# A two-layer mixer trunk on one core: the pooled branch added by accumulating DMAs in six of eight merged tiles of layer 2, and the tiles' first differences tied to an earlier matmul

## The chip, the cores and the metric

The kernel runs on one core of one Trainium2 chip. A time is the device time of one execution in microseconds (us), and the figure that counts is the median over several runs. Times inside an execution come from one profiled run and count from the start of its span. The engines are named as the profile names them: PE (matmul) with PEld (its weight loads), DVE (vector), ACT (scalar), POOL (GpSimd) and SP, which only issues DMAs here.

## The reference

A residual stream of 512 tokens, 16 meta tokens ahead of them and 1024 features passes two layers. Each layer normalises it, projects it, runs a pooled branch and a latent attention branch side by side, gates the two, adds them, and projects the sum back:

```python
y_pool = (pool_mix(u_pool, ...) * silu(z_pool)) @ pool_w_up[l]
o_mla = mla(c_q, c_kv, k_rope, pos, ...)
y_mla = (o_mla * silu(z_mla)) @ mla_w_up[l]
merged = jax.nn.sigmoid(g_pool) * y_pool + jax.nn.sigmoid(g_mla) * y_mla
h_res = h_res + merged @ w_out[l]
```

After layer 2 the meta tokens are dropped. The `+` in `merged` is what this case is about.

## The kernel before

Features lie on the 128 partitions and tokens along a row, so the 1024 features are eight tiles. In layer 2 a merged tile is 128 x 512 (the meta tokens are no longer needed). Every matrix product is done in three matmuls of reduced-precision operands: weight and input are each split into a high part and a low rest, and `mm3` (lines 188, 191 and 192 of `kernel.py`) multiplies high by high, high weight by low input, low weight by high input. The split of a weight chunk is one ACT copy (`whi`, line 183) and one DVE subtraction (`wlo`, line 184); the split of an input tile is the same pair in the helper `split` (lines 297 and 298).

Weights come in 128 x 512 chunks of 256 KB through SP's DMA queue (line 115) into three `raw` buffers (a few into `kh` and `kl`). A `raw` buffer is free for the next chunk when its `wlo` is done, so a late `wlo` on DVE makes a later weight late.

The order of the work. `stream` walks a list of products and yields after each group of matmuls with its estimated length; the list's order is fixed in `register`. `go` is the layer's script: `up(name)` emits products until the named one is done, `fill_now(ns)` emits about that many nanoseconds of matmuls, and in between it emits the work of the other engines. The final order on each engine is then set by the scheduler of the tile framework. Each engine takes its instructions in that order and waits at the first one whose inputs are not there; DMAs are issued by an engine's own queue in the same way. `behind(a, b)` adds a wait of `a` for `b` without a use of data, and `newest[0]` is the last matmul emitted so far. A wait on `newest[0]` thus keeps DVE work from being put too early.

The end of layer 2, where the change is:

- **Products mu0 to mu7** (weights `wmu`, input the attention branch `ogs`, in the profile `q` and `kn`). Each fills a PSUM tile `mm`. Its end is `ev_mu(m)`: line 1049 turns the gate tile `gms[m]` (named `cq`) into (gate + 1) x product, line 1052 adds the gated pooled branch `am[m]`, and `split` makes the inputs `hh`, `hl` of the output product. `am[m]` lives in `xb[:, m]`.
- **`residual(m)`**, eight DMAs on POOL's queue (line 1108), load the residual stream into `xb[:, m]`. Each must wait until `am[m]` there has been read.
- **Output products.** o0, o1, o2 and o3 have a product of their own each, of 24 matmuls of 512 columns. The other four output tiles, in two pairs, are made by `out_pairs`: seven half-size products (256 columns) instead of eight, from sums and differences of weights (prepared earlier, `wsum`) and of the merged tiles. `blend(p)` makes the latter, for p = 7, 6, 5, 4 in turn: for p = 7 tile k minus tile k+4, for k = 0 to 3 (line 1091), for p = 6 lines 1095 and 1096, for p = 4 line 1103. Their splits go into tiles `sq`, `rinv`, `cq` and `u`.
- **Carried halves.** ACT copies some PSUM results out of the banks named `S` into `sv` (line 1130), and POOL adds `sv` to `xb` by accumulating DMAs (line 1131). The outputs `yT` go out on POOL's and SP's queues (line 1068).

In `go` the end reads: all mu products, the eight residual loads, then for each p a `fill_now(2600)` and a blend, then the rest.

Of the kernel before, what the change touches and what calls it, by code (L numbers as in the profile page):

```python
# [14 lines left out]
ALU = mybir.AluOpType  # L15
# [8 lines left out]
T = SEQ + NM  # L24
# [48 lines left out]
def trunk(ctx, tc, xT, pos, win, wkr, wqb, wkb, wvb, wgr, wpu, wmu, wout, gains, const, yT):  # L73
    nc = tc.nc
    pe, act, dve, gp, sp = nc.tensor, nc.scalar, nc.vector, nc.gpsimd, nc.sync
# [66 lines left out]
    def other_loads(made):  # L142
        for k, m in ((2, 0), (4, 1), (6, None)):
            ins = sp.dma_start(xb[:, k:k + 2, :T], xT[:, k:k + 2, :])
            behind(ins, made)
            if m is not None:
                raw = rawt()
                behind(sp.dma_start(raw, win[0, MT_CKV + m, :, 512:1024]), made)
                early.append(raw)
        behind(sp.dma_start(cst, const), made)  # L150
        behind(sp.dma_start(posb[:, :T], pos.partition_broadcast(P)), made)
        dve.tensor_copy(maskw[:, 512 - P:], cst[:, C_MASK:C_MASK + P])
        dve.tensor_copy(identr, ident)
# [97 lines left out]
    def step():  # L251
        c = next(main, None)
        if c is None:
            flush()
            return False
        clk[0] += c
        while pend and pend[0][0] <= clk[0]:
            pend.pop(0)[1]()
        return True

    def after(ns, fn):
        pend.append((clk[0] + ns, fn))
        pend.sort(key=lambda e: e[0])

    def ready():
        while pend and pend[0][0] <= clk[0] + 12000.0:
            pend.pop(0)[1]()
# [5 lines left out]
    def upto(name):  # L273
        while name not in done:
            if not step():
                break
# [10 lines left out]
    def fill_now(ns):  # L287
        end = clk[0] + ns
        while clk[0] < end and step():
            pass  # L290
# [5 lines left out]
    def split(hi, lo, src, a, b):  # L296
        act.activation(hi[:, a:b], src, AF.Copy)  # L297
        dve.tensor_sub(lo[:, a:b], src, hi[:, a:b].bitcast(F32))  # L298
# [42 lines left out]
    def weight_sums(name, w):  # L341
        def made(u, i):
            a, b = w[2 * u], w[2 * u + 1]
            d = wsum[name][u]
            src = {0: (b[:, 0:512], b[:, 512:1024]), 2: (a[:, 0:512], b[:, 0:512]), 1: (a[:, 0:512], d[:, 0, :]),
                   3: (a[:, 512:1024], d[:, 1, :])}
            return d[:, i, :], src[i]

        def copy(d, src):
            behind(sp.dma_start(d, src[0]), earlier(14000))  # L350

        def add(d, src):
            behind(gp.dma_start(d, src[1], accum_op=ALU.add), earlier(4000))  # L353

        for u in range(len(w) // 2):
            for fn, i in ((copy, 0), (copy, 2), (add, 0), (copy, 1), (add, 2), (add, 1), (copy, 3), (add, 3)):
                yield lambda fn=fn, u=u, i=i: fn(*made(u, i))

    class Layer:
# [684 lines left out]
        def ev_mu(self, m):  # L1044
            def ev(ps, a, b):
                if a == self.x0:
                    self.mg[m] = self.hs[m]
                t = self.gms[m][:, a:b]
                dve.scalar_tensor_tensor(out=t, in0=t, scalar=1.0, in1=ps, op0=ALU.add, op1=ALU.mult)
                if b == T:  # L1050
                    t, x0 = self.gms[m], self.x0
                    dve.tensor_add(t[:, x0:T], t[:, x0:T], self.am[m][:, x0:T])
                    split(*self.mg[m], t[:, x0:T], x0, T)
            return ev

# [200 lines left out]
        def go(self, nxt):  # L1256
            l = self.l
            up = lambda name: upto((l, name))
            mix = iter(range(99))
            if l == 0:  # L1260
                for k in range(8):
                    if k in (0, 1, 3, 5):
                        step()
                    self.split_h(k)
                    if k == 0:
                        other_loads(first)
            up("ckv1")
            if l == 0:
                for k in range(8):
                    self.square_x(k)  # L1270
            self.norm_sums()
            up("u1")
            for m in range(2):
                self.mix(m, self.window(m))
            up("u3")
            s2 = self.window(2)
            up("k3")
            s3 = self.window(3)
            up("zp0")
            self.mix(2, s2)  # L1280
            up("zp1")
            self.mix(3, s3)
            self.k_factors()
            if l == 0:
                sums = [*weight_sums(0, [wout[0, m] for m in OUT]), *weight_sums("gp", [win[1, MT_GP + m] for m in range(8)])]
                for i, fn in enumerate(sums):
                    after(3850 * (i + 1), fn)
            up("qr1")
            for s, (a, b) in enumerate(FULL):
                a0 = max(a, self.x0)  # L1290
                self.stat(self.acc[:, a0:b], a0, b, C_CQ, self.acc_last)
            up("qn3")
            self.qk_stats()
            if l == 0:
                fill_now(2600)
            kq = self.prep(0)
            if l == 1:
                for i, fn in enumerate(weight_sums(1, [wout[1, m] for m in OUT])):
                    after(4500 * (i + 1), fn)
            fill_now(2600)  # L1300
            due[0] = None
            prev = None
            for h in range(H):
                kn_ = self.head(h, kq, prev, lambda: self.mixed(next(mix)))
                self.gap()
                self.mixed(next(mix))
                if h + 1 < H:
                    kq = self.prep(h + 1)
                self.pv(prev, (2, 3))
                prev = kn_  # L1310
                self.gap()
                self.mixed(next(mix))
            fill_now(1300)
            self.pv(prev, (0, 1))
            fill_now(2600)
            if not self.last:
                self.meta_queries()
            self.pv(prev, (2, 3))
            up("gm6")
            if self.last:  # L1320
                self.gates_again()
            up("gm7")
            ready()
            if not self.last:
                for p in range(4):
                    self.meta_out(p)
            up("mu7")
            for m in range(8):
                self.residual(m)
            for p in (7, 6, 5, 4):  # L1330
                fill_now(2600)
                self.blend(p)
            up("ob")
            if nxt is not None:
                for k in range(8):
                    nxt.split_h(k)
# [76 lines left out]
```

## Time and profile before

| | us |
|---|---|
| median of 3 runs | 786.03 |
| lowest, highest | 784.74, 787.63 |
| the profiled execution, its own time | 788.06 |
| its span in the profile | 786.2 |

The profiled execution took 2.03 us more than the median, and 1.86 us of its time lie around the span. The granted TensorE clock was 1.0. In the page's first part PE is busy for 774.8 us of the span, DVE for 587.0 and POOL for 230.2. In a timeline row stand start, length, engine, line, operation, output<-input, shape and count; in brackets the idle time ahead of it on its engine and what ended it. A row's length includes a tail that overlaps the next instruction, so the step from start to start is what an instruction costs an engine that is never idle.

### The profile page before, as it was taken

To read this page: it belongs to the slowest core of one execution; us is meant where nothing else is said; L and a number is where in the kernel's file an instruction comes from. 1 tells how busy PE (TensorE), PEld (TensorE's weight loads), DVE (VectorE), ACT (ScalarE), POOL (GpSimd) and SP (SyncE) were. 2 spreads that over 40 slices of the span, in tenths; PEclk is the share of its full clock that TensorE was granted. 3 is DMA by queue.
4 is the path that set the end of the run, shared out by engine and by line. 5 is a ranking of instruction groups with operands and counts; after the bars stand their busy time and mean duration, and the time that the engine had idled before them with its cause. 6 is when DMAs were issued, how large, how long until landed. Compare 5 with 4: busy or idle time off the path is not lost.

```text
span 786.2 us, 15369 instructions
## 1 busy us (share of the span) xinstructions
PE 774.8 (99%) x5469; PEld 711.1 (90%) x5469; DVE 587.0 (75%) x1316; ACT 446.7 (57%) x1022; POOL 230.2 (29%) x319
## 2 busy tenths in 40 slices
PE   9999999999999999999999999999999999999998
PEld 8999899999999999999997898887788899788887
DVE  5848788547778977689764477775997899974984
ACT  8545655645556665545664356455667676654462
POOL 1024514203434342211320245131026235240213
PEclk9999999999999999999999999999999999999999
DMA  6242367765645465565653423435456566562655
GB/s 243 82 97 87 103 163 165 180 154 136 144 120 138 120 135 150 135 187 155 172 151 92 102 81 95 125 88 181 121 132 162 160 168 164 150 212 88 213 148 136
DMA packets 64909, 110.76 MB, mean 141 GB/s; under 512 B 10544, under 2 KB 16560, under 8 KB 64832
## 3 DMA queue, kind: packets, MB, share of 16 engines
q1 hardware_dynamic: 54928, 90.02, 38.4%
q0 software_dynamic: 8896, 17.92, 12.6%
q10 hardware_dynamic: 1008, 1.84, 0.6%
q8 instruction: 43, 0.70, 0.4%
q14 instruction: 34, 0.28, 0.1%
HBM read 100.18 MB, written 22.62 MB: 156 GB/s over the span
## 4 chain that ended last, share of the span: by engine, by line
PE 84%; DVE 6%; DMA 4%; issue 2%; ACT 2%; POOL 0%; SPq 0%; DVEq 0%; ACTq 0%
PE mm L188 24%; PE mm L192 23%; PE mm L191 23%; DVE wlo L184 2%; PE S L188 2%; PE S L191 2%; PE S L192 2%; PE mm L946 2%; DMA raw<-wsumgp 1%; DMA raw<-win 1%; PE o L952 1%; PE o L951 1%; PE S L500 1%; ACT whi L183 1%; DMA raw<-wqb 1%
## 5 line engine op out<-in xcount | busy, mean ns | idle before, releaser
L188 PE MATMUL mm<-hh,whi 128*128 128x264 f32 (+2 forms) x992 | 306.0, 311 | 1.6 <-DVE tmp L637 0.6
L192 PE MATMUL mm<-hh,wlo 128*128 128x264 f32 (+2 forms) x992 | 304.1, 309 | 1.1 <-DVE wlo L184 1.0
L191 PE MATMUL mm<-hl,whi 128*128 128x264 f32 (+2 forms) x992 | 304.5, 308 | 0.0
L184 DVE TENSOR_TENSOR wlo<-raw,whi 128x512 fp32r<-128x512 f32 (+2 forms) x261 | 191.9, 739 | 98.1 <-ACT whi L183 94.3
L183 ACT ACTIVATE whi<-raw 128x512 fp32r<-128x512 f32 (+2 forms) x261 | 156.5, 603 | 165.9 <-PE mm L191 91.0
L188 PEld LDWEIGHTS mm<-hh,whi 128*128 128x128 f32 x992 | 186.2, 188 | 12.9 <-issue 1.2
L192 PEld LDWEIGHTS mm<-hh,wlo 128*128 128x128 f32 x992 | 185.8, 188 | 10.6 <-DVE wlo L184 2.3
L191 PEld LDWEIGHTS mm<-hl,whi 128*128 128x128 f32 x992 | 186.8, 188 | 9.1
L188 PE MATMUL mm<-cq,whi 128*128 128x264 f32 (+2 forms) x140 | 44.2, 316 | 1.3 <-ACT racc L960 0.7
L192 PE MATMUL mm<-cq,wlo 128*128 128x264 f32 (+2 forms) x140 | 43.5, 313 | 0.6 <-DVE wlo L184 0.6
L191 PE MATMUL mm<-cq,whi 128*128 128x264 f32 (+2 forms) x140 | 43.5, 312 | 0.0
L879 DVE CUSTOM_DVE_ANT_0 S<-S,maskw,nqs 128x288 f32<-128x288 f32 (+4 forms) x80 | 38.4, 497 | 2.5 <-PE S L192 2.2
L702 POOL TENSOR_TENSOR racc<-racc,tmp 128x264 f32<-128x264 f32 (+1 forms) x15 | 14.3, 951 | 87.2 <-ACT tmp L701 87.1
L188 PE MATMUL mm<-u,whi 128*128 128x264 f32 (+1 forms) x108 | 35.3, 327 | 0.1
L192 PE MATMUL mm<-u,wlo 128*128 128x264 f32 (+1 forms) x108 | 34.8, 322 | 0.0
L298 DVE TENSOR_TENSOR tl<-mm,th 128x512 fp32r<-128x512 f32 (+1 forms) x64 | 29.2, 481 | 7.4 <-ACT th L297 6.3
L850 POOL TENSOR_TENSOR tmp<-kp,bc 64x528 f32<-64x528 f32 x16 | 25.6, 1602 | 30.5 <-issue 15.4
L353 POOL DMA_DIRECT2D wsum<-wout x8 | 6.9, 859 | 89.0 <-PE mm L192 73.0
L924 POOL TENSOR_TENSOR pm<-pa,rs 128x16 f32<-128x16 f32 x32 | 11.0, 345 | 72.6 <-DVE rs L919 66.7
L926 POOL TENSOR_TENSOR cq<-cq,rs 128x384 f32<-128x384 f32 (+1 forms) x32 | 32.2, 1005 | 0.0
L886 ACT ACTIVATE cq<-S,bia 128x400 f32<-128x400 f32 (+2 forms) x48 | 24.6, 515 | 12.2 <-DVE bia L914 7.2
L297 ACT ACTIVATE th<-mm 128x512 fp32r<-128x512 f32 (+1 forms) x64 | 25.9, 432 | 8.4 <-PE mm L946 7.3
(333 smaller groups left out, 1722.0 us busy)
## 6 DMA issues: line engine op xcount, KB each, us to landing
raw<-win SPq DMA_DIRECT2D x139, 256.0 KB, 3.0
raw<-wout SPq DMA_DIRECT2D x22, 256.0 KB, 3.5
bc<-kdr SPq DMA_DIRECT2D x16, 264.0 KB, 4.2
wsum<-wout SPq DMA_DIRECT2D x16, 256.0 KB, 3.5
raw<-wpu SPq DMA_DIRECT2D x16, 256.0 KB, 3.1
wsumgp<-win SPq DMA_DIRECT2D x16, 256.0 KB, 3.3
raw<-wmu SPq DMA_DIRECT2D x16, 256.0 KB, 2.7
raw<-wsumgp SPq DMA_DIRECT2D x16, 256.0 KB, 3.8
```

The costliest lines, as they stand in the source:

```text
L183: act.activation(hi[:, :n], raw[:, :n], AF.Copy)
L184: dve.tensor_sub(lo[:, :n], raw[:, :n], hi[:, :n].bitcast(F32))
L188: first = pe.matmul(out, wh, xh, start=start, stop=False, skip_group_check=more)
L191: pe.matmul(out, wh, xl, start=False, stop=False, skip_group_check=more)
L192: newest[0] = pe.matmul(out, wl, xh, start=False, stop=stop, skip_group_check=more)
L297: act.activation(hi[:, a:b], src, AF.Copy)
L298: dve.tensor_sub(lo[:, a:b], src, hi[:, a:b].bitcast(F32))
L850: gp.tensor_mul(kf[r0:r0 + 64, :], self.kp[r0:r0 + 64, :], bc[r0:r0 + 64, :])
L879: dve.tensor_tensor_reduce(out=sv, in0=sv, in1=mask, scale=nqs[:, i, h:h + 1], scalar=3e38, op0=ALU.add, op1=ALU.min, accum_out=bia[:, c:c ...
L886: act.activation(pv, sv, AF.Exp, scale=-1.0, bias=bia[:, i:i + 1], accum_out=rs[:, c:c + 1])
L926: gp.tensor_mul(pt[i][:, NM:], pt[i][:, NM:], rs[:, i:i + 1].to_broadcast([P, n - NM]))
L946: pe.transpose(tr[:, P * (i - j):P * (i - j + 1)], pt[i][:, NM + P * j:NM + P * (j + 1)], ident)
```

## The change

Only layer 2 (`self.last`) changes. For merged tiles 0 to 5 the DVE addition of the pooled branch becomes an accumulating DMA on POOL's queue, from SBUF to SBUF, 256 KB each; tiles 6 and 7 keep the DVE addition. And the `fill_now(2600)` ahead of `blend(7)` is left out, so that the differences are tied to the last matmul of mu7 rather than to one of o0, and each later blend to a matmul one such step older.

```diff
                 if b == T:
                     t, x0 = self.gms[m], self.x0
-                    dve.tensor_add(t[:, x0:T], t[:, x0:T], self.am[m][:, x0:T])
+                    if self.last and m < 6:
+                        gp.dma_start(t[:, x0:T], self.am[m][:, x0:T], accum_op=ALU.add)
+                    else:
+                        dve.tensor_add(t[:, x0:T], t[:, x0:T], self.am[m][:, x0:T])
                     split(*self.mg[m], t[:, x0:T], x0, T)
...
             for p in (7, 6, 5, 4):
-                fill_now(2600)
+                if p != 7 or not self.last:
+                    fill_now(2600)
                 self.blend(p)
```

The lines behind the edits move by 3 and 4: 1091 becomes 1094, 1095 becomes 1098, 1108 becomes 1111, 1130 becomes 1133.

What follows is the order of instructions, without times. On POOL's queue, at the end of layer 2, there stood eight residual loads in a row, each behind the DVE addition of its tile. Of the changed kernel these are the rows at that place (line 1053 is the accumulating DMA, and `cq_1885`, `1886`, `1887`, `1888`, `1889`, `1890` are merged tiles 0 to 5; line 1111 the residual load):

```order
L1053 DMA cq_1885_9611<-xb 128x512
L1053 DMA cq_1886_9613<-xb 128x512
L1053 DMA cq_1887_9615<-xb 128x512
L1111 DMA xb<-scr 128x512
L1053 DMA cq_1888_9617<-xb 128x512
L1111 DMA xb<-scr 128x512
L1053 DMA cq_1889_9619<-xb 128x512
L1111 DMA xb<-scr 128x512 x3
L1053 DMA cq_1890_9621<-xb 128x512
L1111 DMA xb<-scr 128x512 x3
```

The first residual load waits for tile 0's accumulating DMA to land, the second for tile 1's; the three in one row are those of tiles 2, 3 and 6, which wait for tile 2's and tile 3's DMAs and tile 6's DVE addition. The DMA of tile 3 stands behind the first residual load, that of tile 5 behind the three.

On DVE, around the last mu products, the kernel before has these rows (`mm_9824` is mu7; `cq_1874` and `cq_1894` are merged tiles 6 and 7; `hl` the low parts; line 1091 the differences of p = 7):

```order
L1049 SCALAR_TENSOR_TENSOR cq_1894_9647<-cq_1894_9647,mm_9824 128x512
L184 TENSOR_TENSOR wlo_10084<-kl_10081,whi_10083 128x512
L298 TENSOR_TENSOR hl_15_141<-cq_1889_9619,hh_14_140 128x512
L1052 TENSOR_TENSOR cq_1890_9621<-cq_1890_9621,xb 128x512
L1052 TENSOR_TENSOR cq_1894_9647<-cq_1894_9647,xb 128x512
L298 TENSOR_TENSOR hl_19_145<-cq_1874_9577,hh_18_144 128x512
L184 TENSOR_TENSOR wlo_9926<-raw_9923,whi_9925 128x512
L184 TENSOR_TENSOR wlo_9961<-raw_9958,whi_9960 128x512
L298 TENSOR_TENSOR hl_17_143<-cq_1890_9621,hh_16_142 128x512
L298 TENSOR_TENSOR hl_21_147<-cq_1894_9647,hh_20_146 128x512
L1091 TENSOR_TENSOR cq_1889_9619<-cq_1885_9611,cq_1889_9619 128x256
```

The changed kernel has at the same place:

```order
L1049 SCALAR_TENSOR_TENSOR cq_1894_9647<-cq_1894_9647,mm_9824 128x512
L298 TENSOR_TENSOR hl_15_141<-cq_1889_9619,hh_14_140 128x512
L1094 TENSOR_TENSOR cq_1874_9577<-cq_1887_9615,cq_1874_9577 128x256
L184 TENSOR_TENSOR wlo_10084<-kl_10081,whi_10083 128x512
L1055 TENSOR_TENSOR cq_1894_9647<-cq_1894_9647,xb 128x512
L1094 TENSOR_TENSOR cq_1889_9619<-cq_1885_9611,cq_1889_9619 128x256
L298 TENSOR_TENSOR hl_21_147<-cq_1894_9647,hh_20_146 128x512
L298 TENSOR_TENSOR sq_9850<-cq_1889_9619,sq_9849 128x256
L1094 TENSOR_TENSOR cq_1894_9647<-cq_1888_9617,cq_1894_9647 128x256
L184 TENSOR_TENSOR wlo_9942<-raw_9939,whi_9941 128x512
L298 TENSOR_TENSOR hl_17_143<-cq_1890_9621,hh_16_142 128x512
```

The addition for tile 5 is gone from DVE, `hl_17_143` (tile 5's low part) now waits for a DMA, and three of the four differences stand ahead of it.

On PE, at the products of p = 7 and p = 6 of the pairs, the kernel before has (`mm_10149` and `mm_10129` are the banks of p = 7; the `S` banks those of p = 6, reused after an ACT copy of line 1130):

```order
L188 MATMUL mm_10149<-sq_9880,whi_10125 128x256
L191 MATMUL mm_10149<-sq_9881,whi_10125 128x256
L188 MATMUL S_10043<-cq_1952_9895,whi_10145 128x256
L191 MATMUL S_10043<-u_1953_9896,whi_10145 128x256
L188 MATMUL S_10065<-cq_1952_9895,whi_10165 128x256
```

and the changed kernel:

```order
L191 MATMUL mm_10149<-sq_9858,whi_10125 128x256
L192 MATMUL mm_10149<-sq_9857,wlo_10126 128x256
L188 MATMUL mm_10149<-sq_9861,whi_10125 128x256
L191 MATMUL mm_10149<-sq_9862,whi_10125 128x256
L192 MATMUL mm_10149<-sq_9861,wlo_10126 128x256
L188 MATMUL S_10043<-cq_1945_9864,whi_10145 128x256
L191 MATMUL S_10043<-u_1946_9865,whi_10145 128x256
```

Ten more matmuls of `mm_10149` (all twelve of that product) now stand ahead of the first matmul into the reused `S` bank.

## Prediction

> **What bounds the kernel now.** The page first: its first part says which engine is full, the chain of waits which one set the end.
>
> ```profile
> PE 774.8 (99%) x5469; PEld 711.1 (90%) x5469; DVE 587.0 (75%) x1316; ACT 446.7 (57%) x1022; POOL 230.2 (29%) x319
> ...
> PE 84%; DVE 6%; DMA 4%; issue 2%; ACT 2%; POOL 0%; SPq 0%; DVEq 0%; ACTq 0%
> ```
>
> PE is busy for 774.8 of 786.2 us. The change takes no matmul away, so it can win only PE's idle time, and of that only what lies behind the edit. The view of busy time by stretches, laid over the end of layer 2 (busy time and count for PE, PEld, DVE, ACT and POOL, then granted clock, DMA share and GB/s), shows how much that is:
>
> ```profile
> 726.50:738.70 12.20, 12.20 (x55) 9.87 (x54) 12.15 (x21) 6.23 (x11) 2.55 (x5) 1.00 0.57 187
> 738.70:750.00 11.30, 11.30 (x50) 9.14 (x49) 8.82 (x15) 4.73 (x8) 1.86 (x4) 1.00 0.68 219
> 750.00:760.00 10.00, 10.00 (x63) 8.93 (x62) 10.00 (x27) 7.04 (x17) 1.10 (x2) 1.00 0.33 96
> 760.00:770.00 10.00, 8.84 (x72) 8.43 (x72) 10.00 (x24) 5.97 (x14) 3.98 (x6) 1.00 0.71 197
> 770.00:780.00 10.00, 10.00 (x63) 8.95 (x63) 4.11 (x7) 2.44 (x5) 3.90 (x7) 1.00 0.57 118
> ```
>
> DVE is full from 726.5 to 738.7, and again from 750 to 770. PE does not care, except in one stretch: 760 to 770, where it is idle for 1.16 us. The timeline finds the two places:
>
> ```profile
> 762.81 0.38 PE L188 MATMUL S<-cq,whi 128*128 128x256 f32 x1 [0.92 <-ACT sv L1130]
> ...
> 768.77 0.39 PE L188 MATMUL S<-cq,whi 128*128 128x256 f32 x1 [0.24 <-ACT sv L1130]
> ```
>
> Both are the first matmul into an `S` bank that ACT must empty first. Why ACT was late at the first place, by the timelines of ACT, SP and DVE:
>
> ```profile
> 761.86 0.63 ACT L183 ACTIVATE whi<-raw 128x512 fp32r<-128x512 f32 x1 [1.96 <-DMA raw<-wsum]
> 762.39 0.64 ACT L1130 ACTIVATE sv<-S 128x256 f32<-128x256 f32 x2
> ...
> 751.81 7.41 SPq L115 DMA_DIRECT2D raw<-wsum  x3
> ...
> 756.24 0.69 DVE L184 TENSOR_TENSOR wlo<-raw,whi 128x512 fp32r<-128x512 f32 x1
> ```
>
> The copies of line 1130 stand behind a weight copy that waited for its DMA. That DMA could go only once DVE had freed its buffer, at 756.24 + 0.69 = 756.93, and landed about 4.9 us later. So DVE's backlog after 750 is what PE paid for, and the prize is **1.16 us** at most.
>
> **The DVE side of the change.** The timeline of DVE where the additions stand, and where the differences do:
>
> ```profile
> 726.55 1.28 DVE L1049 SCALAR_TENSOR_TENSOR cq<-cq,mm 128x512 f32<-128x512 f32 x2 [2.88 <-PE mm L192]
> 727.76 0.68 DVE L184 TENSOR_TENSOR wlo<-raw,whi 128x512 fp32r<-128x512 f32 x1
> 728.36 0.69 DVE L1052 TENSOR_TENSOR cq<-cq,xb 128x512 f32<-128x512 f32 x1
> 728.96 0.68 DVE L1049 SCALAR_TENSOR_TENSOR cq<-cq,mm 128x512 f32<-128x512 f32 x1
> ...
> 749.74 1.43 DVE L1091 TENSOR_TENSOR cq<-cq,cq 128x256 f32<-128x256 f32 x4 [2.48 <-PE mm L192]
> ...
> 752.36 0.42 DVE L298 TENSOR_TENSOR sq<-cq,sq 128x256 fp32r<-128x256 f32 x1
> 752.70 0.42 DVE L1095 TENSOR_TENSOR cq<-cq 128x256 f32<-128x256 f32 x1
> ```
>
> From start to start a 512-column instruction costs a full DVE 0.60 us, a 256-column one 0.34. Six additions less are 6 x 0.60 = 3.6 us of DVE between 728 and 743, but PE is not idle there, so by itself this wins nothing. The second edit matters more: the differences waited 2.48 us for a matmul of o0, with DVE idle, just ahead of its backlog. They now need only mu7 and their own tiles, and go into that hole. The second blend takes over the first one's matmul, the low-weight product of o0 with tile 5. PE's rows give the pace:
>
> ```profile
> 738.65 0.40 PE L192 MATMUL mm<-q,wlo 128*128 128x512 f32 x1
> 738.88 0.39 PE L188 MATMUL mm<-hh,whi 128*128 128x512 f32 x1
> ...
> 755.57 0.28 PE L188 MATMUL S<-hh,whi 128*128 128x256 f32 x1
> 755.69 0.28 PE L191 MATMUL S<-hl,whi 128*128 128x256 f32 x1
> ```
>
> A 512-column matmul takes 0.232 us of PE (72 of them from 738.88 to 755.57), a 256-column one 0.118. In the new order that matmul is the 36th of the output products: 738.88 + 35 x 0.232 + 0.4 = 747.4. From there DVE has nineteen instructions ahead of the `wlo` that frees the buffer, sixteen of 256 columns and three of 512: 16 x 0.34 + 3 x 0.60 = 7.2, so it starts at 754.6 instead of 756.24. The weight then lands near 760.2, and ACT's copies of `S`, 0.53 + 0.64 us on, end near 761.4. PE wants the bank at 762.81 - 0.92 = 761.9 plus the ten matmuls that moved ahead of it, 1.2 us: 763.1. The 0.92 us go, with 1.7 us to spare, and the 0.24 behind them, on the same engines, I count as gone too. No other idle time of PE is late next: PE is the bound up to the last product, whose order the change leaves.
>
> **The POOL side.** Each removed addition becomes a DMA, and three things queue up. On ACT, the copy `hh` of a tile waits for the landing, and weight copies stand behind it. On DVE, `hl` waits for `hh`, and `wlo` rows stand behind it. On POOL, the residual load of a tile waits for the landing of that tile's DMA, and the DMA of a later tile stands behind the load. That makes a chain: tile 0 lands, its residual load goes, tile 3's DMA goes and lands, three residual loads go (the third waits for tile 6's addition on DVE), tile 5's DMA goes and lands. PE waits for tile 5.
>
> No row shows this very DMA: 256 KB, added from SBUF to SBUF. The nearest, by the answers on lines 1131 (`xb<-sv`, added from SBUF to SBUF, but 128 or 132 KB) and 353 (256 KB, added in DRAM), and a plain load on POOL's queue:
>
> ```profile
> L1131 POOL DMA_DIRECT2D xb<-sv x12: 862/893/1178, 380.7 to 776.6; - x12
> ...
> DMA to landing us min/median/max: 2.7/3.8/5.1
> ...
> DMA to landing us min/median/max: 4.2/5.6/7.6
> ...
> 729.41 0.62 POOL L1108 DMA_DIRECT2D xb<-scr  x1 [30.76 <-DVE cq L1052]
> ```
>
> The first landing row belongs to line 1131, the second to line 353. So the landing takes from 2.7 us (half the bytes) to 7.6 us (the worst in DRAM). It also depends on company. The queues:
>
> ```profile
> q1 hardware_dynamic: 54928, 90.02, 38.4%
> q0 software_dynamic: 8896, 17.92, 12.6%
> ```
>
> POOL's queue takes 12.6% of 786.2 us for 17.92 MB, 5.5 us of all sixteen engines per MB, so 1.4 us for each new DMA and 8.7 us for six. From 726.5 to 750 the DMA engines are busy for 12.2 x 0.57 + 11.3 x 0.68 = 14.6 of 23.5 us; with the new ones 23.3, nearly full. I take 4.0 us for tile 0, which starts where the engines are still idle, and 5.5 us, next to the DRAM median, for tiles 3 and 5.
>
> Now the sum. Line 1049 of tile 0 ends at 727.24, so its DMA goes at 727.3. Tile 5 lands at 727.3 + 4.0 + 0.6 (a residual load's issue) + 5.5 + 2 x 0.6 + 5.5 = 744.1. PE wants `hh` of tile 5 as the 30th matmul, at 738.88 + 29 x 0.232 = 745.6; an ACT copy takes 0.6, so the tile must land by 744.9. Only 0.8 us are to spare, and ACT and DVE carry weight copies between, so I charge 0.3 us of stall. In other words: tile 5 lands at 729.1 plus three landings, and PE begins to stall when the three exceed **15.8 us**.
>
> By the Trainium skill ("DMA: Bandwidth & Descriptors", section on the anatomy of one DMA on the SWDGE path) a DMA of POOL's queue takes about 2.0 us plus its bytes over 436 GB/s: 2.6 us for 256 KB as an estimate, 7.8 for the chain, and the full 1.16 us would be won. The trace disagrees for adding DMAs: the best of line 353's took 4.2 us and the median 5.6, and the measurement decides.
>
> **Sum.** 788.06 - 1.16 + 0.3 = 787.2 for an execution like the profiled one, which lies 2.03 above the median. On the scale of the medians: 786.03 - 0.86, so **785.2 us**.
>
> **The rivals.**
>
> *The gain is given back.* At 5.6 us for each of the three, the DRAM median, the sum is 16.8, one us over the point, and the tiles' copies on ACT lose some tenths more; net 0 to -0.2: 786.0. The same time results if the differences bring nothing, because the weight is late for another reason, such as full DMA engines. For this speaks the DMA sum of 23.3 in 23.5 us; against it that the first DMA starts in a quiet stretch, and that line 1131's, from SBUF, land faster.
>
> *The chain on POOL makes it slower.* One landing beyond 15.8 us in sum is one us of PE stall, since nothing behind PE can make it up; beyond 15.8 + 1.16 = 17.0, a mean of 5.7 us, the kernel is slower than before. At a mean of 6.0: 18 - 15.8 - 1.2 = +1.0, 787.0; at the worst row's 7.6: 22.8 - 15.8 - 1.2 = +5.8, 791.8.
>
> *POOL is hindered by DVE.* Were descriptors written more slowly while DVE works, each issue would lengthen; the longest of line 1131's is 1.18 us against a median of 0.89, so 0.3 on each of three links, 0.9 in sum, which just uses up the 0.8 to spare: 785.5. Against it: with DVE busy for 12.15 of 12.20 us, POOL's five issues took 2.55 us, 0.51 each. The Trainium skill ("GPSIMD Engine Reference", section 1, Specifications) has GpSimd contend with DVE instructions of two SBUF inputs, as all of these are; by that rule this rival holds, and the trace's plain loads do not agree.
>
> **How the numbers follow.** The forecast, -1.2 to -0.4 with the third rival in it: 0.50. Given back, -0.4 to +0.5: 0.25. Slower by 0.5 to 3.9 us: 0.16. Slower by more than 3.9 us, 0.5% and about what a measurement of this kernel can tell from no change: 0.07, for which the mean landing must pass 6.9 us. Faster by more than 3.9 us: 0.02, as PE has only 1.16 us to give. So 0.02, 0.91 and 0.07. The range ends above at a mean landing near 6.5 us (19.5 - 15.8 - 1.2 = +2.5), below at the full gain, 784.9; the runs of before spread from 784.74 to 787.63, so I allow the median of a few runs 0.9 on the lower side: **784.0 to 788.5**.
>
> **What would show it.** Right: between 760 and 770 PE's busy time is 10.0; the first blend's rows carry no wait for PE and lie ahead of 747; the adding DMAs land in 4 to 5.5 us. Wrong: a wait of PE between 743 and 749 for `hh` or `hl` of a tile or for a weight copy behind one; landings of 6 us or more; POOL's residual loads waiting for them; or a new wait of PE near 767, where the `S` banks are reused a second time.

## The result, and the profile after

The changed kernel takes **791.05 us** (median of six runs, 789.33 to 792.59) against 785.71 for the kernel before beside it (six runs, 784.74 to 787.63): the ratio is 1.0065, 95% interval 1.0053 to 1.0077. It is slower by 5.3 us; 785.2 was predicted, with a range to 788.5.

The profiled execution took 791.76 us, with a span of 789.6. The first instruction of the place in question, line 1049 of tile 0, starts at 726.87 instead of 726.55, before anything differs. From there to the end of the span it is 62.7 us, before 59.65: **the tail is 3.1 us longer** in this execution. The view by stretches, as shown of before (busy time and count for PE, PEld, DVE, ACT and POOL, granted clock, DMA share, GB/s):

```profile
726.50:738.70 12.20, 12.20 (x54) 9.90 (x53) 9.04 (x15) 5.36 (x9) 6.21 (x8) 1.00 0.79 174
738.70:750.00 11.30, 8.41 (x33) 5.58 (x31) 8.84 (x17) 5.36 (x10) 3.63 (x6) 1.00 1.01 299
...
760.00:770.00 10.00, 10.00 (x79) 9.69 (x78) 9.03 (x21) 5.79 (x12) 2.37 (x3) 1.00 0.76 207
770.00:780.00 10.00, 9.47 (x60) 8.41 (x59) 4.73 (x8) 4.25 (x9) 4.32 (x6) 1.00 0.57 132
```

The 1.16 us between 760 and 770 are gone, as forecast, but PE now stands for 2.9 us between 738.7 and 750, where the DMA engines are full (1.01 of their time by this view), and for 0.5 us after 770. PE's timeline has the three places before 750:

```profile
741.98 0.73 PE L188 MATMUL mm<-hh,whi 128*128 128x512 f32 x2 [0.52 <-ACT hh L297]
...
748.60 0.50 PE L188 MATMUL mm<-hh,whi 128*128 128x512 f32 x1 [2.10 <-ACT whi L183]
...
749.61 1.02 PE L188 MATMUL mm<-hh,whi 128*128 128x512 f32 x2 [0.27 <-ACT hh L297]
```

The chain of work that ended last is now this (start, length, what); before, it ran along PE here:

```profile
727.97 4.71 DMA cq<-xb
732.72 0.59 issue
733.30 0.56 POOL xb L1111
733.86 7.41 DMA cq<-xb
741.27 0.40 issue
741.67 1.08 POOL xb L1111 x2
742.76 6.14 DMA cq<-xb
748.92 0.64 ACT hh L297
749.61 0.49 PE mm L188
```

It is the chain on POOL that the prediction describes: tile 0 lands, a residual load goes, tile 3's DMA goes and lands, residual loads go, tile 5's DMA goes and lands. Its three landings are 4.7, 7.4 and 6.1 us, 18.3 in sum. At its end PE starts tile 5's first matmul, the 30th of the output products, at 749.61. The first of them started at 739.20, so without a wait the 30th would have come at 739.20 + 29 x 0.232 = 745.9: **PE is 3.7 us late there**. (Idle times in the rows add up to only 2.9, because the matmuls next to a wait also take 0.34 or 0.52 us instead of 0.23.) The answer on line 1053 gives all six:

```profile
DMA to landing us min/median/max: 4.7/6.6/7.4
```

The longest of PE's waits, 2.10 us, came another way, through tile 4. It lies inside the 3.7: an earlier tile 4 would only have let PE wait longer for tile 5. Rows of POOL, ACT and DVE in order of time:

```profile
737.08 0.88 POOL L1053 DMA_DIRECT2D cq<-xb  x1 [1.03 <-DVE hl L298]
744.16 0.63 ACT L297 ACTIVATE hh<-cq 128x512 fp32r<-128x512 f32 x1 [1.20 <-DMA cq<-xb]
744.83 0.69 DVE L298 TENSOR_TENSOR hl<-cq,hh 128x512 fp32r<-128x512 f32 x1 [0.38 <-ACT hh L297]
745.44 0.42 DVE L1094 TENSOR_TENSOR cq<-cq,cq 128x256 f32<-128x256 f32 x1
745.77 0.68 DVE L184 TENSOR_TENSOR wlo<-kl,whi 128x512 fp32r<-128x512 f32 x1
746.38 0.68 DVE L1055 TENSOR_TENSOR cq<-cq,xb 128x512 f32<-128x512 f32 x1
747.09 0.63 ACT L297 ACTIVATE hh<-cq 128x512 fp32r<-128x512 f32 x1 [1.78 <-DVE cq L1055]
747.93 0.61 ACT L183 ACTIVATE whi<-raw 128x512 fp32r<-128x512 f32 x1
```

Tile 4's DMA, whose line 1049 was done at 731.8, goes only at 737.08, because two residual loads and tile 3's DMA stand ahead of it on POOL, and lands at 744.1. On DVE its low part, a difference that the second edit put there, a weight's low half and the addition of tile 7 follow one another; ACT takes tile 7's high part, and only then the weight copy for which PE waits.

### The profile page after: what moved, and what is told of

The parts are those of the page before. It is cut to its first block, busy times and chain, and to the rows that moved or that the text cites. A ratio compares the mean times of both kernels' runs of the same rounds, so it can differ in the third digit from the quotient of the medians.

```text
span 789.6 us, 15373 instructions
## 1 busy us (share of the span) xinstructions
PE 777.0 (98%) x5469; PEld 712.5 (90%) x5469; DVE 583.2 (74%) x1310; ACT 447.1 (57%) x1022; POOL 236.1 (30%) x325
## 3 DMA queue, kind: packets, MB, share of 16 engines
q10 hardware_dynamic: 1008, 1.84, 0.6%
## 4 chain that ended last, share of the span: by engine, by line
PE 81%; DMA 6%; issue 5%; DVE 4%; POOL 1%; ACT 1%; SPq 0%; DVEq 0%; ACTq 0%; POOLq 0%
PE mm L188 23%; PE mm L192 23%; PE mm L191 22%; PE S L191 2%; PE S L188 2%; PE S L192 2%; DMA cq<-xb 2%; DMA raw<-win 2%; PE mm L946 2%; DVE wlo L184 1%; PE o L952 1%; PE o L951 1%; PE S L500 1%; DMA raw<-wqb 1%; DMA xb<-sv 1%
## 5 line engine op out<-in xcount | busy, mean ns | idle before, releaser
L184 DVE TENSOR_TENSOR wlo<-raw,whi 128x512 fp32r<-128x512 f32 (+2 forms) x261 | 189.8, 731 | 97.7 <-ACT whi L183 93.9
L191 PE MATMUL mm<-kn,whi 128*128 128x264 f32 (+1 forms) x96 | 30.6, 320 | 0.0
```

The source lines that it names most:

```text
L184: dve.tensor_sub(lo[:, :n], raw[:, :n], hi[:, :n].bitcast(F32))
L191: pe.matmul(out, wh, xl, start=False, stop=False, skip_group_check=more)
```

## The experiments

Each ran beside the kernel before. The tail is from the start of the first line 1049 to the end of the span, in the one profiled execution; before it is 59.65.

| kernel | us | before | ratio (95%) | tail | PE's waits from 740 to 760 |
|---|---|---|---|---|---|
| after, first execution | 791.05 | 785.71 | 1.0065 (1.0053 to 1.0077) | 62.7 | 0.52, 2.10, 0.27 |
| the tie alone | 786.44 | 785.42 | 1.0012 (1.0000 to 1.0024) | 59.2 | none |
| the additions alone | 791.35 | 785.42 | 1.0067 (1.0047 to 1.0088) | 64.9 | 1.45, 2.31 |
| idle additions | 787.80 | 785.42 | 1.0023 (1.0011 to 1.0035) | 60.5 | 0.59 |
| loads late | 788.53 | 785.42 | 1.0034 (1.0023 to 1.0045) | 60.3 | 0.24, 0.33, 0.78 |
| before again | 785.56 | 785.65 | 1.0000 (0.9985 to 1.0016) | 59.2 | none |
| POOL computes | 788.07 | 785.65 | 1.0028 (1.0014 to 1.0043) | 61.3 | 1.42, 0.21 |
| first three tiles | 787.29 | 785.65 | 1.0012 (0.9997 to 1.0028) | 59.3 | 0.56 |
| loads late, more space | 788.21 | 785.65 | 1.0025 (1.0010 to 1.0040) | 60.9 | 1.84, 0.33 |
| after again | 791.51 | 786.33 | 1.0063 (1.0039 to 1.0088) | 64.6 | 1.65, 1.43 |
| last three tiles | 790.63 | 786.33 | 1.0053 (1.0037 to 1.0069) | 64.0 | 3.23, 0.39 |
| no loads | 786.22 | 786.33 | 0.9995 (0.9981 to 1.0008) | 60.1 | 0.56, 0.33 |
| loads later | 787.23 | 786.87 | 1.0007 (0.9993 to 1.0022) | 59.9 | 0.28, 1.30 |
| last three, loads later | 785.45 | 786.18 | 0.9992 (0.9979 to 1.0005) | 59.4 | 0.77 |
| loads later, mended | 787.00 | 786.18 | 1.0010 (1.0000 to 1.0021) | 61.5 | 0.82, 0.33, 1.39 |

**The two edits apart.** The tie alone keeps the second edit and puts line 1052 back; the additions alone keep the first:

```diff
-                if p != 7 or not self.last:
-                    fill_now(2600)
+                fill_now(2600)
```

> Only the second edit: the differences are tied to the older matmul, all eight additions stay on DVE. If PE loses its time to the landings of the adding DMAs (the main theory), this one has no such DMA and can only win: 0 to 1.2 us below the kernel before, 784.5 to 785.7. If full DMA engines are the cause (first rival), the same, since no transfer is added. If the tie itself is the cause, because the differences now stand on DVE ahead of the low weight halves (second rival), it is slower by most of the 5.3 us, 789 to 791, with PE waiting for a weight copy near 748.

> Only the first edit: six adding DMAs, the differences tied as before. Main theory (landings): the POOL chain is as long as in the kernel after, so 4 to 6 us slower than before, 789.5 to 791.5, PE waiting between 741 and 750. First rival (full DMA engines): the same. Second rival (the tie): within 1 us of before, 785 to 786.7.

The first edit costs all of it (1.0067); the second by itself wins nothing. The trace of the tie alone shows why. Rows of DVE, ACT, then PE:

```profile
747.76 1.43 DVE L1095 TENSOR_TENSOR cq<-cq 128x256 f32<-128x256 f32 x4 [1.00 <-PE mm L192]
...
754.94 0.68 DVE L184 TENSOR_TENSOR wlo<-raw,whi 128x512 fp32r<-128x512 f32 x1
...
759.72 0.63 ACT L183 ACTIVATE whi<-raw 128x512 fp32r<-128x512 f32 x1 [1.48 <-PE mm L192]
760.25 0.64 ACT L1130 ACTIVATE sv<-S 128x256 f32<-128x256 f32 x2
...
760.67 0.39 PE L188 MATMUL S<-cq,whi 128*128 128x256 f32 x1 [0.98 <-ACT sv L1130]
```

The gap is still there. This execution's first line 1049 starts at 724.56, so times here compare with those of before when counted from there. The second blend starts 23.2 us after it, where the first blend stood in before (749.74 - 726.55), and not at the forecast 20.9 (747.4): with this order of PE's matmuls the one it is tied to is no earlier. The `wlo` that frees the buffer starts at 30.4 instead of 29.7, so the weight, whose DMA goes at 755.6 and takes 4.0 us, lands no sooner than in before (35.1 against 35.2 us). The trace puts the weight copy's wait down to a matmul of PE, which ended about 0.1 us behind that landing.

**Do the bytes cost, or the waiting for them?** All eight additions stay on DVE; the six adding DMAs go beside them into tiles that nobody reads (shown against the tie alone; the lines that set these tiles up and clear them are left out):

```diff
+                    if self.last and m < 6:
+                        behind(gp.dma_start(self.idle[m][:, x0:T], self.am[m][:, x0:T], accum_op=ALU.add), ins)
                     dve.tensor_add(t[:, x0:T], t[:, x0:T], self.am[m][:, x0:T])
```

> The tie, and all eight additions on DVE; beside them the six adding DMAs are issued at the places where the kernel after has them, from the same source, into six tiles that nobody reads afterwards. So the transfers and POOL's queue are those of the kernel after, but hh of a tile does not wait for them (the residual loads still do). Main theory: within 0.7 us of the run with the tie alone, no PE wait for hh between 739 and 750. First rival (full DMA engines make the weights late): 4 to 6 us slower than before, 790 to 791, with PE waits for weight copies whose own DMA came late.

Both theories get a part. The time is 2.4 us above before and some 1.4 above the tie alone (with overlapping intervals), and a PE wait of 0.59 us for a weight's low half appears. The bytes do slow their neighbours: the answer on line 115, the weight loads between 722 and 760, of before and of this kernel:

```profile
DMA to landing us min/median/max: 3.0/3.7/4.8
```

```profile
DMA to landing us min/median/max: 3.3/4.9/6.5
```

With the tie alone the median is 3.5, in the kernel after 5.4. But the larger part of the 5.3 us is not in the bytes alone. (The residual loads still wait for these DMAs here, so POOL's chain is in this run too, with nobody but the loads behind it.)

**The chain on POOL taken apart.** The residual loads of layer 2 are issued after blend 7, tied to a matmul 1.3 us into the output products:

```diff
+                if p == 6 and self.last:
+                    end = clk[0] + 2600
+                    fill_now(1300)
+                    mid = newest[0]
+                    fill_to(end)
...
+                    for m in range(8):
+                        behind(self.residual(m), mid)
```

> As the kernel after, but the eight residual loads are tied to a matmul 1.3 us into the output products, so that on POOL all six adding DMAs stand ahead of them and none waits for a landing. Main theory in its form with the chain on POOL: tiles 3 and 4 go right behind their line 1049 and land by about 739, tile 5 by about 746; PE's 2.9 us of waits between 741 and 750 shrink to 1 us or less, and the time is 785 to 787.5. First rival: the same bytes in the same stretch, 789.5 or more. Second rival: 789 or more, with the same PE wait behind the differences.

PE's waits before 750 shrink to 0.57 us, and somewhat under half of the loss goes, but the time expected is not reached. The profiled execution, 786.91 us, was one of the fastest of the twelve (786.84 to 790.04), so its trace does not show all that the median of 788.53 holds. POOL's timeline shows two things:

```profile
725.64 2.71 POOL L1053 DMA_DIRECT2D cq<-xb  x3 [29.01 <-DVE cq L1049]
730.46 0.86 POOL L1053 DMA_DIRECT2D cq<-xb  x1 [2.11 <-issue]
733.09 0.86 POOL L1053 DMA_DIRECT2D cq<-xb  x1 [1.76 <-DVE wlo L184]
739.06 0.89 POOL L1053 DMA_DIRECT2D cq<-xb  x1 [5.11 <-DVE cq L1049]
740.88 3.84 POOL L1111 DMA_DIRECT2D xb<-scr  x7 [0.93 <-PE mm L192]
```

The fourth DMA goes when ACT sees tile 0 landed (730.18), the fifth when it sees tile 1 (732.81), though no wait in the program says so. And the seven loads now go in one burst at 741, beside the weights: a weight copy then waits 1.9 us for its DMA and PE 0.78 us behind it, at 753.27.

The scale for such small differences is the kernel before, run as if it were another:

```diff
+# a comment line
```

> The kernel before itself, with one comment line more: a scale for small differences. In the first four experiments the time outside the span was 2.1 us in every changed kernel and 1.8 in every run of before, and the kernel with the tie alone is 1.0 us slower although its tail in the trace is 0.4 shorter. If that much belongs to how a second program is measured beside the first, this one shows it too: 0.3 to 1.0 us slower, 2.1 us outside its span. If it belongs to the changed programs: 785.0 to 785.8, 1.8 us outside the span.

It is 1.0000, and 1.84 us lie around its span as in before. So the 2.1 us around the span of the kernel after and of some of the others are theirs: 0.3 us that no view explains. In this execution the gap that was to be won is 0.43 and 0.24 us, not 0.92 and 0.24.

The fourth and fifth DMA, with more descriptor space:

```diff
-    nc = bacc.Bacc("TRN2", target_bir_lowering=False, num_devices=1, dynamic_dma_scratch_size=1024)
+    nc = bacc.Bacc("TRN2", target_bir_lowering=False, num_devices=1, dynamic_dma_scratch_size=1600)
```

> As the run with the residual loads moved back, and the descriptor space of POOL's queue enlarged from 1024 to 1600; every engine's order is the same. In that run the fourth and the fifth adding DMA were issued only when the first and the second had landed (2.1 and 1.8 us of POOL idle that no wait explains). If the descriptor space holds three of them, here the fourth goes right behind its line 1049, about 1.5 us earlier, and the fifth waits for the first landing instead of the second. If that wait is part of the cost, the time falls by 0.5 to 1.5 us against that run, to 787.0 to 788.0; if the filled DMA engines set when the tiles land, the issues move, each landing takes longer by as much, and the time stays within 0.5 us of 788.5.

Counted from the first line 1049, the fourth goes at 4.05 us instead of 5.92 and the fifth at 5.25 instead of 8.55: 1024 holds three of these DMAs. The time hardly moves (1.0025 against 1.0034); the longest landing grows from 7.4 to 8.0 us. Issuing earlier into full engines gains nothing that these runs can tell.

**Which tiles.** The first three, then the last three by DMA alone:

```diff
-                    if self.last and m < 6:
+                    if self.last and m < 3:
```

> As the kernel after, but only tiles 0, 1 and 2 are added by DMA, the others on DVE. These three are issued one behind the other, so no link of a chain on POOL, and land by about 736, before PE starts the output products near 739. Theory (what costs is the late end of the chain, tiles 3 to 5): no PE wait before 750, and the time of the run with the tie alone plus about half of what six idle transfers cost there (1.4 us), 786.4 to 787.6. Rival (the copies that wait for the first landings hold up ACT and DVE, and that is never made good): 788.5 or more, half of the way or more.

```diff
-                    if self.last and m < 6:
+                    if self.last and 2 < m < 6:
```

> As the kernel after, but only tiles 3, 4 and 5 are added by DMA, tiles 0, 1 and 2 on DVE. Now no adding DMA stands ahead of them. If it was the chain (the landings of the first three ahead of the last three) that made them late, they go right behind their line 1049, land in about 5 us, and only tile 5, issued near 739 to 740, is late by 0 to 1 us: 786 to 788. If PE simply wants these three tiles too soon for any DMA, the chain being beside the point, the stall is that of the kernel after, 2 to 3 us, and the time 789.5 or more.

The first three cost nothing that can be told from the tie alone (1.0012), though they take as long to land (median 6.6 us): the last had landed by 736.8, and PE wants the first only near 739. The last three cost most of it. By the letter of the expectation that would speak against the chain, but its premise was wrong, as POOL's timeline shows: a residual load stands behind each of the three here, so the chain is there, in its purest form.

```profile
728.97 0.87 POOL L1053 DMA_DIRECT2D cq<-xb  x1 [1.22 <-DVE cq L1049]
...
734.25 0.54 POOL L1111 DMA_DIRECT2D xb<-scr  x1 [2.98 <-DMA cq<-xb]
734.89 0.90 POOL L1053 DMA_DIRECT2D cq<-xb  x1
740.46 0.55 POOL L1111 DMA_DIRECT2D xb<-scr  x1 [4.68 <-DMA cq<-xb]
741.09 0.88 POOL L1053 DMA_DIRECT2D cq<-xb  x1
...
746.41 1.13 POOL L1111 DMA_DIRECT2D xb<-scr  x2 [3.88 <-DMA cq<-xb]
```

Three landings of about 5 us, one after the other. So this run did not decide, and another had to: the same three tiles, with the loads behind all three DMAs and later still:

```diff
+                if p == 6 and self.last:
+                    end = clk[0] + 2600
+                    fill_now(1300)
+                    behind(self.residual(0), newest[0])
+                    fill_to(end)
...
+                if p == 5 and self.last:
+                    for m in range(1, 8):
+                        behind(self.residual(m), newest[0])
```

> Tiles 3, 4 and 5 by DMA, the others on DVE, and all residual loads behind the adding DMAs on POOL (the first tied to the 11th or so of the output products, the others to one 2.6 us later). So no landing stands between two of the three. If the chain made them late: tile 4's DMA goes right behind its line 1049 instead of behind tile 3's landing, PE's 3.2 us of wait for hh fall to 1 us or less, no loss of clock, 786 to 788. If these tiles are wanted too soon for any DMA: a PE wait of 2 us or more, 789.5 or more, as with the loads between them.

POOL's timeline, and the landings:

```profile
728.59 0.92 POOL L1053 DMA_DIRECT2D cq<-xb  x1 [32.60 <-DVE cq L1049]
731.60 0.88 POOL L1053 DMA_DIRECT2D cq<-xb  x1 [2.09 <-DVE cq L1049]
736.40 0.87 POOL L1053 DMA_DIRECT2D cq<-xb  x1 [3.93 <-DVE cq L1049]
```

```profile
DMA to landing us min/median/max: 4.1/4.3/5.1
```

Each DMA now waits only for its own line 1049, and 5.2 us of time are gone between these two kernels (790.63 and 785.45; ratios to before 1.0053 and 0.9992, intervals apart). These are the same three DMAs, with the residual loads between them or behind them. Moving the loads took both things away, the waits between the DMAs and the loads' bytes beside them, but the rows tell them apart. Counted from the first line 1049 (724.27 and 723.90), tile 4's DMA goes at 7.7 us instead of 10.6 and tile 5's at 12.5 instead of 16.8, while the median landing falls only from 4.9 to 4.3. **So for these three tiles it is the chain**, the time of the issue and not the length of the landing.

**And the bytes of the loads.** First the six DMAs without any residual load:

```diff
-            for m in range(8):
+            for m in range(0 if self.last else 8):
                 self.residual(m)
```

> As the kernel after, but the eight residual loads of layer 2 are left out, so the residual isn't added and the output is another. Nothing then stands between the adding DMAs on POOL but their own descriptor space, and 2 MB less go through the DMA engines in the stretch. If the filled engines make the landings long, they shrink here to a median of 5 us or less, and with them the stall to 1 us or less: 785.5 to 787. If the adding DMA is slow by itself, the median stays above 6 us and the time at 788 or more, as in the run with the loads moved back.

This kernel leaves the residual out of its output. The landings shrink little (3.8/5.8/7.4 us; the descriptor space and the other five adding DMAs remain), but the time is that of before. So six adding DMAs can be borne, if neither the loads between them nor the loads' bytes beside them come on top. Then with the loads, late enough:

```diff
+                if p == 5 and self.last:
+                    for m in range(8):
+                        behind(self.residual(m), newest[0])
```

> As the run with the residual loads moved back, but tied to a matmul 2.6 us later (the 22nd of the output products, near 744), so that most of their bytes move after 748, into the stretch from 750 to 760 in which the DMA engines of the kernel before are busy for a third of the time. Nothing is left out. If the two things that make the landings late are the waits between the DMAs on POOL and the bytes of the residual loads beside them, this comes near the run without the loads: 785.5 to 787.3, with PE waiting less than 1 us between 741 and 755. If the loads cost wherever they stand, because the first output products' additions to the residual then wait for them, it stays at 788 to 789, with DVE's line 1062 waiting for a load near 755.

In this kernel tile 0's load comes behind the addition that it should precede, so that tile's output is another; the work is the same. The mended one has the edit of the run with the last three tiles above, for all six:

> The run with the residual loads moved later still, mended: tile 0's load is tied 1.3 us into the output products, ahead of its addition, the other seven near 744. All six additions by DMA, nothing left out or changed. If the POOL chain and the loads' bytes beside the adding DMAs are the whole cause: within 1.2 us of before on either side, 785.3 to 787.7, no PE wait over 1.5 us before 760. If something of the loss hangs on the adding DMAs whatever stands around them: 788.5 or more.

1.0007 and 1.0010: 5.3 us become less than 1. What is left is of the size of the interval; in the second trace stands a wait of 1.39 us for a weight copy at 753.87. No version here beats the kernel before by more than the measurement can tell; the best, the last three tiles with the loads later, is at 0.9992 (0.9979 to 1.0005).

**POOL adds by itself.** No DMA and no landing:

```diff
-                        gp.dma_start(t[:, x0:T], self.am[m][:, x0:T], accum_op=ALU.add)
+                        gp.tensor_add(t[:, x0:T], t[:, x0:T], self.am[m][:, x0:T])
```

> As the kernel after, but POOL computes the six additions itself instead of issuing six adding DMAs. An addition of 128x512 took POOL 1.1 to 1.8 us in the kernel before (lines 926, 702 and 534). So the sum of a tile is there some 2 us after line 1049 instead of 5 to 7, POOL's queue waits for no landing, and no byte is added to the DMA engines. Theory of the landings: no PE wait before 750, the time of the run with the tie alone or better, 785 to 786.7. Rival, the edit costs because DVE's order changes as the additions leave it: 789 or more.

Wrong, for a reason of its own. Rows of POOL and DVE in the same time:

```profile
728.98 1.33 POOL L1053 TENSOR_TENSOR cq<-cq,xb 128x512 f32<-128x512 f32 x1
729.47 3.22 DVE L184 TENSOR_TENSOR wlo<-raw,whi 128x512 fp32r<-128x512 f32 x1
730.83 1.30 POOL L1053 TENSOR_TENSOR cq<-cq,xb 128x512 f32<-128x512 f32 x1
```

A `wlo` that takes 0.68 us elsewhere lasts 3.22 beside two of POOL's additions, and tile 5's addition on POOL lasts 2.60. So the run can't judge the landings.

**The kernel after once more**, with a comment line more (its line numbers are one higher):

> The kernel after once more, with one comment line more: a second profiled execution. Theory: PE waits some 3 us between 741 and 751 behind copies that waited for landings, tiles 3 to 5 land 6 us or more after their issue, and the fifth adding DMA is issued only when the third has landed. The five timed runs showed a mean granted clock of 0.998 and the profiled one 0.999; if the stall sometimes costs the clock, this execution may show matmuls at 0.5 behind it, as the run with the additions alone did (12 matmuls 0.43 us apart instead of 0.23). Time 789.5 to 792.5.

Nearly the same waits, 3.1 us, but a tail 1.8 us longer than in the first execution. PE's clock, by stretches:

```profile
742.00:744.00 2.00, 1.98 (x9) 1.28 (x7) 2.00 (x4) 0.34 (x1) 0.35 (x1) 1.00 0.95 210
744.00:746.00 2.00, 0.37 (x2) 0.30 (x2) 1.64 (x5) 1.46 (x3) 0.54 (x1) 1.00 1.07 282
746.00:748.00 2.00, 0.57 (x3) 0.19 (x1) 0.96 (x3) 0.87 (x2) 0.50 (x1) 0.61 1.03 372
748.00:750.00 2.00, 2.00 (x5) 1.49 (x6) 1.42 (x3) 0.82 (x3) 0.04 (x1) 0.50 0.79 253
750.00:752.00 2.00, 2.00 (x6) 1.54 (x6) 0.70 (x3) 0.42 (x2) 0.00 (x0) 0.50 0.51 148
752.00:754.00 2.00, 2.00 (x8) 1.59 (x7) 2.00 (x8) 1.36 (x5) 0.00 (x0) 0.68 0.00 0
```

Once the waits are over PE is full, and at **half its clock**: matmuls are 0.43 us apart instead of 0.23 until 753.2. From 747.81 to 753.19 twelve matmuls take 5.4 us, which at 0.232 would take 2.8: 2.6 us lost. With the waits, 3.1 less the 1.16 of before, that makes 4.5 of the 4.9 us by which this tail is longer than before's. The price shows in the six runs of the additions alone, too: 788.55 us at a mean clock of 1.000, 790.08 and 790.59 at 0.998, 792.11 to 792.55 at 0.996. Five of the first six runs of the kernel after show 0.998, and those of before 0.999 to 1.000. As an estimate, 0.002 of 789 us is 3.2 us at half clock, so these runs lost up to 1.6 us.

## Why the prediction was wrong, point by point

*What bounds the kernel.* Right: PE, and no gain beyond its idle time.

*The prize.* Right for the kernel after, as far as its trace shows, though not for the second edit by itself. The gap between 760 and 770 is gone, and once PE's own lateness is taken off, the second blend and the weight that had been late came when the forecast said. The blend is tied to the 36th matmul of the output products and starts 24.9 us after the first line 1049, forecast 20.9, at a place where PE is 4.1 late; the DMA goes at 759.7, that is 32.8, forecast 28.7. With the tie alone 0.98 us stay, because that matmul is about the 46th there; the forecast did not say that it needs both edits. The gap is gone with the additions alone as well, where PE is later still, so the kernel after can't show that the tie won it. The runs of the first three tiles and of the last three with the loads later point to it: the tie is in both, PE waits no more than 0.8 us, and the gap is gone. But 0.5 us came back in the kernel after behind line 1129, which waited for a carried half to land.

*The DVE side.* Right that the differences lose their wait for PE. That 3.6 us less DVE win nothing by themselves was not tested apart from the landings. Only two of the four differences start ahead of 747, counted from the first line 1049. With the tie alone the other two start 1.0 and 1.4 us past it, in the kernel after 1.4 and 3.5 us, since there they read tiles that landed late. What the first of them passes was not counted: it stands between tile 4's low part and tile 7's addition, on the path of the 2.10 us.

*The POOL side.* The mechanism and the rows were right; the sizes were not. **"I take 4.0 us for tile 0, which starts where the engines are still idle, and 5.5 us, next to the DRAM median, for tiles 3 and 5"** is the step that failed: they took 4.7, 7.4 and 6.1, 3.3 us more than the 15.0 assumed. A second term was too small. Between the landings the prediction allows only for issues, but 1.2 us more went by until POOL took the next DMA (the first went 0.4 us later behind line 1049, tile 3's 1.2 us behind tile 0's landing instead of 0.6, tile 5's 1.5 instead of 1.2). So tile 5 landed at 748.9, which is 4.8 us behind the 744.1 of the prediction: 3.3 of landings, 1.2 of links and 0.3 by which this execution started later. The stall was 3.7 us where 0.3 was charged. The 15.8 us that the three landings may take without a stall were thus too generous by 1.2: by that rule 18.3 would have meant 2.5. That this lies near the 2.9 us of idle time in PE's rows is luck. The prediction had worked out that the DMA engines would be full for 23.3 of 23.5 us, and took a median all the same. It also looked at tile 5 alone; tiles 3 and 4 made PE wait first, though tile 5 had the last word. By the page's formula in the Trainium skill ("DMA: Bandwidth & Descriptors", the anatomy of one DMA on the SWDGE path), 2.6 us as an estimate, the whole prize would have been won; no landing of a 256 KB adding DMA here was under 3.5 us, and the measurement decides.

*What was not in the sum.* Three things: the descriptor space, which holds three of these DMAs and, by the pattern of the runs with the loads late, held back tile 4's for 1.0 of its 5.3 us; the clock; and 0.3 us around the span. In the first execution 3.7 us of lateness, less the 1.16 won, plus the 0.5 after 770 make the 3.1 us by which the tail is longer, to within some tenths. With 0.3 around the span and the estimate of up to 1.6 for the clock, that is 5.0 of the 5.3 us.

*The rivals.* "The chain on POOL makes it slower" is what happened, at a mean of 6.1 us, for which its rule gives 787.3 (18.3 - 15.8 - 1.2 = +1.3); it lacks the 1.2 us of links and takes it that a microsecond of stall costs no clock. "POOL is hindered by DVE" did not happen to DMAs: a plain load's issue on POOL took 0.55 us in the median, before 0.54. It did happen to computation, in both directions (3.22 and 2.60 us above), which the Trainium skill has in "GPSIMD Engine Reference", section 1, Specifications: SBUF interfaces shared with the vector engine, contention with DVE instructions of two SBUF inputs. The trace agrees there, for `wlo`. (The prediction counts all DVE rows of the stretch among these, but line 1049 reads a product in PSUM.)

*What would show it.* Three of the four signs named for "wrong" came: PE waits between 743 and 749 for a weight copy behind a tile's `hh`, landings over 6 us, and residual loads on POOL that wait for them (8.9 us in sum). The fourth, a wait near 767, did not. Of the signs for "right" one came, PE busy for all of 760 to 770, and half of another, no wait for PE in the first blend's rows; they belong to the prize and say nothing of the chain.

## What to carry to other kernels

A DMA in place of an instruction puts a wait into every in-order queue that touches its data, so look for the next DMA of that queue behind such a wait: the chain that forms adds up landings, and the last three tiles' DMAs issued without it cost nothing that could be measured. Where the sum of the bytes fills the DMA engines, take the worst landing of the nearest row and not its median. And where PE is the bound, expect that a stall of three microseconds can cost up to nearly twice its length: in one of the two profiled executions of this kernel the clock went with it, 2.6 us on 3.1, and in the other it did not.

## What the runs showed of the hardware that was not expected

- **The clock.** After 1.65 and 1.43 us of idle PE with two matmuls between (after again), 1.45 and 2.31 (the additions alone), or 3.23 and 0.39 (last three tiles), the granted clock fell to 0.50, and by steps of 0.25 us it stayed there from 746.4 to 753.3, from 747.6 to 754.5, and from 748.5 to 751.9: 6.8, 6.8 and 3.4 us. After 2.10 and 0.27, or 1.84 and 0.33, it did not fall. The Trainium skill ("TensorE: Matmul & The Clock Gate", Part 1) has half rate after an idle window of about 3.4 us and full rate after a busy one, the windows running freely. The ratio and the lengths agree. But no idle window was needed: in the 3.41 us ahead of each fall PE was busy for 1.68, 0.98 and 1.40 us. In the first of these the second wait began only as the clock fell, so one wait of 1.65 us seems to have been enough. What share of idle time it takes is not shown.
- **Descriptor space.** With 1024, three adding DMAs of 256 KB were outstanding on POOL's queue and the fourth waited without a semaphore, up to 2.8 us; with 1600 the fourth did not. Seven plain loads of 256 KB went back to back with 1024.
- **Adding DMAs, 256 KB, SBUF to SBUF**, landed in 3.5 to 8.0 us; the medians of the runs lay between 4.3 and 6.7.
